# Rows of 4 KB for the first pieces, and neighbourhood attention by two pairs of heads at a time

## The chip, the core and the metric

The program runs on one core of one Trainium2 chip, and the metric is device time in microseconds (us). The core has TensorE (PE, matrix products; its weight loads are PEld), VectorE (DVE), ScalarE (ACT), GpSimd (POOL) and SyncE (SP), which here issues nearly all transfers. The engines take their own instructions in order and wait for one another by semaphores. Products land in PSUM, eight banks of 128 x 512 fp32 here; all else lies in SBUF.

## The reference

A trunk of two layers over 256 tokens of 1024 values, all in fp32. Three mixers work side by side on one input projection:

```python
for l in range(DEPTH):
    x = x + 0.5 * swiglu(rms_norm(x, ffn1_norm[l]), w1, w3, w2)         # hidden width 2816
    z = rms_norm(x, mix_norm[l]) @ w_in[l]                              # 6752 columns
    y_na  = neighborhood_attention(rms_norm(q), rms_norm(k), v, na_rpb[l])   # 8 heads of 64
    y_gla = rms_norm(gla_bidirectional(gq, gk, gv, g_f, g_b)) * silu(gr)     # 4 heads
    y_mla = mla_attention(c_q, c_kv, k_rope, ...)                            # 4 heads
    mixed = gt[0] * (y_na @ w_br_na[l]) + gt[1] * (y_gla @ w_br_gla[l]) + gt[2] * (y_mla @ w_br_mla[l])
    x = x + mixed @ w_out[l]
    x = x + 0.5 * swiglu(rms_norm(x, ffn2_norm[l]), w1, w3, w2)

# neighborhood_attention: tokens on a grid of 4 rows x 64 columns; a block of 16 columns of
# queries sees a band of 32 columns in all 4 rows, and a window of 16 columns inside it
s = einsum('brjqhd,brjkhd->bhrjqk', qg, kg) * d ** -0.5
s = where(mask, s + bias, -1e30)
o = einsum('bhrjqk,brjkhd->brjqhd', softmax(s), vg)
```

## The kernel before, in words

All weights come as "units", 128 partitions by 2048 values (1 MB, rows of 8 KB), in the order of their use, into three buffers called raw. Every unit is split into a high and a low half (hl, four buffers): ScalarE rounds the high half (L143), VectorE takes the rest (L149). Every fp32 product is then three products of halves, and nearly all go through one helper (`mm`, L373). SP has eight transfers under way at most: each waits for the eighth before it.

The main program is a row of projections. After each burst of products on TensorE it calls `tick`, which issues the next splits and lets each small task, a Python generator, go one step. So the order on every engine is fixed when the program is built, and the small products of attention stand between bursts of projections; a visit of TensorE to such a task is what it does there between two bursts. A task that ends a step with `yield n` is called again after n ticks.

Working tiles of 128 x 512 (`s2`) come from a pool of 31 buffers (`S2_BUFS`, L28). A new tile takes the buffer that was freed first, and the instruction that writes it waits for the last reader of the tile that had it. PSUM has four banks for projections (`acc`) and four for the small tasks (`ta`).

The start is written out by hand (`start_first`, L303 to L367). The transposed input xT (eight chunks, called k, of 128 x 256) and the first three units come in 20 transfers of one or two chunks, into 16 tiles of the pool. They are worked off in the groups `(0, 1), (1, 2), (2, 4), (4, 6), (6, 8)` of k: L344 and L347 make the halves of xT with the norm's gain, L352 and L353 those of the units, and per k each unit has six small products (144 in all, 128 x 256), into a bank of its own.

The mixer is at L1116 to L1209. In its order: the MLA and gate inputs, then NA's v, q, k projections; a task normalises q and k (`ev_nqk`: L638 and L640), another transposes them (`na_tr`: L691). `mla_chain` (L851 to L935) has scores for a pair of heads, their softmax (L905, L906, L913), transposes of the probabilities (`p_trans`, L676, split by L247 and L248) and products with v. Then come the projections of GLA's gq and gk (L1133 to L1147), where GLA's gate exponentials (L993 to L995) fall, and four projections of gates, each four bursts of 12 products of 408 columns, among which `na_chain` (L711 to L784) runs, spawned at L1148.

`na_chain` takes the four pairs of heads one at a time, in six steps. Step i loads the bias of pair i + 1 (256 KB), computes scores of pair i (L736, eight small products, 16 records in the trace, into half of two banks), adds the bias and takes the maximum (L743), takes the exponential (L750), divides on GpSimd (L772), transposes pair i - 1 (L778) and multiplies pair i - 2 with v (L761).

Of the kernel before, what the change touches and what calls it, by code (L numbers as in the profile page):

```python
# [46 lines left out]
def body(tc, T):  # L47
# [3 lines left out]
    with ctx:  # L51
# [9 lines left out]
        def s2(shape=(128, 512), dt=F32):  # L61
            return sp.tile(list(shape), dt, name="s2", tag="s2", bufs=S2_BUFS)
# [240 lines left out]
        def start_first():  # L303
# [8 lines left out]
            xr = [s2() for _ in range(4)]  # L312
            rw = [[s2() for _ in range(4)] for _ in range(FIRST_R)]
            groups = ((0, 1), (1, 2), (2, 4), (4, 6), (6, 8))
            at = lambda tiles, a, b: tiles[a // 2][:, a % 2 * 256:a % 2 * 256 + (b - a) * 256]
            for a, b in groups:
                nc.sync.dma_start(out=at(xr, a, b), in_=T["xT"][:, a:b, :])  # L317
                for j in range(FIRST_R):
                    nc.sync.dma_start(out=at(rw[j], a, b), in_=units[j][0][:, a * 256:b * 256])  # L319
# [21 lines left out]
            for a, b in groups:  # L341
                sl = slice(a * 256, b * 256)
                for k in range(a, b):
                    ACT.activation(out=xT[:, :, 0, k, :], in_=at(xr, k, k + 1).rearrange("p (t n) -> p t n", t=2),  # L344
                                   func=AF.Copy, scale=gcol[:, k:k + 1])
                for k in range(a, b):
                    DVE.scalar_tensor_tensor(out=xT[:, :, 1, k, :],  # L347
                                             in0=at(xr, k, k + 1).rearrange("p (t n) -> p t n", t=2),
                                             scalar=gcol[:, k:k + 1], in1=xT[:, :, 0, k, :].bitcast(F32),
                                             op0=ALU.mult, op1=ALU.subtract)  # L350
                for j in range(FIRST_R):
                    ACT.activation(out=hls[j][:, 0, sl], in_=at(rw[j], a, b), func=AF.Copy)  # L352
                    DVE.tensor_tensor(out=hls[j][:, 1, sl], in0=at(rw[j], a, b), in1=hls[j][:, 0, sl].bitcast(F32),  # L353
                                      op=ALU.subtract)
                    for k in range(a, b):
                        part(accs[j], hls[j], k)
# [199 lines left out]
        def mixer(l, norms, after, prefetch):  # L556
# [153 lines left out]

            def na_chain(deps):  # L711
                for d in deps:
                    finish(d)
                bias = {}

                def bias_load(p):
                    if p < 4:
                        bias[p] = s2((128, 2, 2, 128))
                        nc.sync.dma_start(out=bias[p], in_=W["bias"][p])
                bias_load(0)  # L720
                yield 1
                Ps, PTs, sums = {}, {}, {}
                for i in range(4 + 2):
                    if i < 4:
                        bias_load(i + 1)
                        q, k = naT["q", i // 2], naT["k", i // 2]
                        ps = [at_t()[:, :256].rearrange("p (g n) -> p g n", g=2) for _ in range(2)]
                        for g in range(2):
                            for s in range(2):
                                r = slice(s * 64, s * 64 + 64)  # L730
                                for jj in range(2):
                                    j = 2 * g + jj
                                    k0 = min(max(16 * j - 8, 0), 32)
                                    kj = k[r, i % 2, :].rearrange("p (r c) -> p r c", r=4)[:, :, k0:k0 + 32]
                                    o = ps[s][jj * 64:jj * 64 + 64, g, :].rearrange("p (r c) -> p r c", r=4)
                                    mm(o, q[r, i % 2, j * 64:j * 64 + 64], kj, True, True)  # L736
                        m, sm_ = small(4), small(4)
                        P = s2((128, 2, 2, 128))
                        Ps[i], sums[i] = P, sm_
                        b = bias.pop(i)  # L740
                        for s in range(2):
                            for g in range(2):
                                DVE.tensor_tensor_reduce(out=P[:, s, g, :], in0=ps[s][:, g, :], in1=b[:, s, g, :],  # L743
                                                         scale=1.0, scalar=-3.0e38, op0=ALU.add, op1=ALU.max,
                                                         accum_out=m[:, 2 * s + g:2 * s + g + 1])
                        DVE.tensor_scalar(m, m, -1.0, None, op0=ALU.mult)
                        for s in range(2):
                            for g in range(2):
                                e = slice(2 * s + g, 2 * s + g + 1)
                                ACT.activation(out=P[:, s, g, :], in_=P[:, s, g, :], func=AF.Exp,  # L750
                                               bias=m[:, e], accum_out=sm_[:, e])
                    yield 1
                    if i >= 2:
                        p = i - 2
                        ps = at_t()
                        PT = PTs.pop(p)
                        for j in range(4):
                            for s in range(2):
                                h = 2 * p + s
                                o = ps[s * 64:s * 64 + 64, :256].rearrange("p (r c) -> p c r", r=4)  # L760
                                mm(o[:, 16 * j:16 * j + 16, :], nav[j][:, h * 64:h * 64 + 64],  # L761
                                   PT[:, s, j // 2, (j % 2) * 64:(j % 2) * 64 + 64], True, True)
                        if p % 2 == 0:
                            yT["na", p // 2] = (s2(dt=F32R), s2(dt=F32R))
                        hi, lo = yT["na", p // 2]
                        sl = slice((p % 2) * 256, (p % 2) * 256 + 256)
                        split_bank(ps[:, :256], hi[:, sl], lo[:, sl])
                    if i < 4:
                        rs = small(4)
                        DVE.reciprocal(rs, sums[i])  # L770
                        P4 = Ps[i].rearrange("p s g n -> p (s g) n")
                        POOL.tensor_tensor(out=P4, in0=P4, in1=rs[:, :, None].to_broadcast([128, 4, 128]), op=ALU.mult)  # L772
                    if 1 <= i < 5:
                        P = Ps.pop(i - 1)
                        ps = tr_t().rearrange("p (s g n) -> p s g n", s=2, g=2)
                        for s in range(2):
                            for g in range(2):
                                PE.transpose(ps[:, s, g, :], P[:, s, g, :], idt)  # L778
                        PT = PTs[i - 1] = s2((128, 2, 2, 128))
                        if i % 2:  # L780
                            ACT.activation(out=PT, in_=ps, func=AF.Copy)
                        else:
                            DVE.tensor_copy(PT, ps)
                    yield 1  # L784
# [347 lines left out]
            for j, nm in enumerate(("q", "k")):  # L1132
# [236 lines left out]
```

## Time and profile before

| | us |
|---|---|
| median of 3 timed runs (lowest, highest) | 1243.21 (1243.17, 1244.23) |
| profiled execution, its own time | 1244.47 |
| its span | 1242.7 |
| TensorE busy | 1235.9 |
| VectorE busy | 891.0 |
| ScalarE busy | 709.8 |
| GpSimd busy | 219.7 |
| bytes moved | 228.58 MB, mean 184 GB/s |

The span is what the profiler saw of the program; the execution's own time has a little more around it. Busy shares are averages over stages, so a wait is judged where it stands. A timeline row is a run of equal instructions: its start, the time from its first start to its last end, and in brackets how long the engine stood before it and for whom. "Clock" is what the throttle granted TensorE, 1.00 for 2.4 GHz and 0.50 for 1.2 GHz.

### The profile page before, as it was taken

How to read it: one execution, taken by the hardware profiler on the slowest of the kernel's cores; microseconds unless marked ns; L12 is line 12 of the kernel's file. 1: busy time of each engine (PE TensorE's matmuls, PEld its weight loads, DVE VectorE, ACT ScalarE, POOL GpSimd, SP SyncE). 2: the span in 40 equal slices, each digit the busy share in tenths (PEclk: the TensorE clock that was granted, in tenths of full speed). 3: DMA queues.
4: the chain of work that ended last, by engine and by line, in shares of the span. 5: the costliest groups of instructions: out<-in, count | busy, mean ns of one | idle time of the engine just before them, and what ended most of it. 6: DMA issues, size and time to landing. Idle time of an engine off the chain costs nothing.

```text
span 1242.7 us, 18139 instructions
## 1 busy us (share of the span) xinstructions
PE 1235.9 (99%) x7020; PEld 1060.4 (85%) x7020; DVE 891.0 (72%) x1390; ACT 709.8 (57%) x1308; POOL 219.7 (18%) x165
## 2 busy tenths in 40 slices
PE   9999999999999999999999999999999999999998
PEld 8888888889988888888888888888899888888887
DVE  5888736779767778887378886475896677788862
ACT  6655535657665366555365655355686654656541
POOL 0222101132112112220012220021322030122200
PEclk9999999999999999999999999999999999999999
DMA  8655644562543545556355556347526435555560
GB/s 307 232 177 196 239 168 161 181 219 94 198 170 138 201 172 202 177 196 238 136 189 208 203 174 250 120 163 250 175 88 211 170 138 188 191 195 192 181 237 34
DMA packets 39350, 228.58 MB, mean 184 GB/s; under 512 B 5920, under 2 KB 8224, under 8 KB 14816
## 3 DMA queue, kind: packets, MB, share of 16 engines
q1 hardware_dynamic: 39120, 227.42, 52.0%
q8 instruction: 55, 0.90, 0.3%
q14 instruction: 31, 0.25, 0.1%
q10 hardware_dynamic: 144, 0.00, 0.0%
HBM read 224.26 MB, written 1.05 MB: 181 GB/s over the span
## 4 chain that ended last, share of the span: by engine, by line
PE 99%; DMA 0%; SPq 0%; ACT 0%; DVE 0%; issue 0%; DVEq 0%
PE acc L373 80%; PE ta L373 15%; PE ta L691 1%; PE ta L264 1%; DMA s<-in_xT 0%; PE ta L778 0%; PE ta L1199 0%; PE ta L676 0%; SPq L319 0%; PE ta L1014 0%; PE ta L608 0%; PE ta L299 0%; PE ta L469 0%; ACT xT L344 0%; SPq L317 0%; DVE hl L353 0%
## 5 line engine op out<-in xcount | busy, mean ns | idle before, releaser
L149 DVE TENSOR_TENSOR hl<-raw,hl 128x1024 fp32r<-128x1024 f32 (+1 forms) x418 | 560.2, 1381 | 94.1 <-ACT hl L143 83.8
L143 ACT ACTIVATE hl<-raw 128x1024 fp32r<-128x1024 f32 (+1 forms) x418 | 412.9, 1041 | 106.1 <-PE ta L373 87.3
L373 PE MATMUL acc<-xT,hl 128*128 128x256 f32 (+1 forms) x2720 | 466.6, 334 | 0.0
L373 PEld LDWEIGHTS acc<-xT,hl 128*128 128x128 f32 x2720 | 407.9, 188 | 56.3
L373 PE MATMUL acc<-hl,xT 128*128 128x512 f32 (+1 forms) x1584 | 362.9, 384 | 0.0
L373 PEld LDWEIGHTS acc<-hl,xT 128*128 128x128 f32 x1584 | 291.8, 188 | 47.4 <-issue 2.1
L373 PE MATMUL acc<-hl,s 128*128 128x512 f32 x816 | 193.7, 391 | 0.0
L373 PEld LDWEIGHTS acc<-hl,s 128*128 128x128 f32 x816 | 152.6, 188 | 31.7 <-issue 0.3
L483 POOL TENSOR_TENSOR s<-s,rsb 128x512 f32<-128x512 f32 x79 | 109.7, 1388 | 352.1 <-DVE s L482 352.1
L373 PE MATMUL ta<-hl,s 128*128 128x512 f32 (+1 forms) x624 | 148.0, 387 | 0.0
L373 PEld LDWEIGHTS ta<-hl,s 128*128 128x128 f32 x624 | 116.3, 188 | 22.4
L492 ACT ACTIVATE s<-s 128x256 fp32r<-128x256 f32 x82 | 34.0, 417 | 168.1 <-DVE s L490 168.1
L482 DVE TENSOR_TENSOR s<-acc,s 128x256 f32<-128x256 f32 x158 | 59.7, 419 | 58.5 <-ACT s L481 58.5
L569 POOL TENSOR_TENSOR sm<-sm,mhalf 128x4 f32<-128x4 f32 (+2 forms) x24 | 36.7, 1531 | 190.8 <-DVE sm L573 190.8
L285 POOL TENSOR_TENSOR sm<-sm,mhalf 128x1 f32<-128x1 f32 x12 | 14.1, 1175 | 299.0 <-DVE sm L284 299.0
L481 ACT ACTIVATE s<-acc 128x256 f32<-128x256 f32 x158 | 50.6, 372 | 0.0
L247 ACT ACTIVATE s<-ta 128x512 fp32r<-128x512 f32 (+1 forms) x46 | 22.9, 532 | 36.5 <-PE ta L691 16.9
L267 ACT ACTIVATE xT<-ta,gain 128x128 fp32r<-128x128 f32 x80 | 22.8, 368 | 36.3 <-PE ta L264 36.3
L248 DVE TENSOR_TENSOR s<-ta,s 128x512 fp32r<-128x512 f32 (+1 forms) x46 | 26.6, 603 | 22.9 <-ACT s L247 22.5
L488 ACT ACTIVATE s<-s 128x256 f32<-128x256 f32 x82 | 34.2, 419 | 11.5 <-POOL s L483 1.2
L373 PEld LDWEIGHTS ta<-s,s 64*64 64x64 f32 (+3 forms) x720 | 30.4, 145 | 6.9 <-issue 5.9
L373 PE MATMUL ta<-s,s 64*64 64x128 f32 (+4 forms) x720 | 35.9, 261 | 0.0
(160 smaller groups left out, 678.6 us busy)
## 6 DMA issues: line engine op xcount, KB each, us to landing
raw<-in_l_f_w SPq DMA_DIRECT2D x123, 1024.0 KB, 4.8
raw<-in_l_in_g SPq DMA_DIRECT2D x16, 816.0 KB, 4.4
raw<-in_l_in_late SPq DMA_DIRECT2D x8, 1024.0 KB, 4.8
raw<-in_l_out SPq DMA_DIRECT2D x8, 1024.0 KB, 4.8
raw<-in_l_f_up SPq DMA_DIRECT2D x6, 1024.0 KB, 4.8
raw<-in_l_in_m SPq DMA_DIRECT2D x4, 1024.0 KB, 4.8
raw<-in_l_in_gr SPq DMA_DIRECT2D x4, 1024.0 KB, 4.8
raw<-in_l_in_r SPq DMA_DIRECT2D x4, 1024.0 KB, 4.7
```

The costliest lines, as they stand in the source:

```text
L143: ACT.activation(out=hls[j][:, 0, sl], in_=raws[j][:, sl], func=AF.Copy)
L149: DVE.tensor_tensor(out=hl[:, 1, sl], in0=r[:, sl], in1=hl[:, 0, sl].bitcast(F32), op=ALU.subtract)
L247: ACT.activation(out=hi, in_=ps, func=AF.Copy)
L248: DVE.tensor_tensor(out=lo, in0=ps, in1=hi.bitcast(F32), op=ALU.subtract)
L267: ACT.activation(out=xT[:, t, 0, kk, :], in_=ps[:, k * 128:(k + 1) * 128], func=AF.Copy, scale=G[:, kk:kk + 1])
L373: PE.matmul(out=out, lhsT=lhsT, rhs=rhs, start=start, stop=stop, skip_group_check=True)
L481: ACT.activation(out=g[:, j, :], in_=a[j][:, 256:], func=AF.Copy)
L482: DVE.tensor_tensor(out=g[:, j, :], in0=a[j][:, :256], in1=g[:, j, :], op=ALU.add)
L483: POOL.tensor_tensor(out=g, in0=g, in1=rb[:, None, :].to_broadcast([128, 2, 256]), op=ALU.mult)
L488: ACT.activation(out=g[:, 0, :], in_=g[:, 0, :], func=AF.Silu)
L492: ACT.activation(out=o[:, 0, :], in_=g[:, 0, :], func=AF.Copy)
L569: POOL.tensor_tensor(out=r[:, :n], in0=ss[:, :n], in1=mhalf[:, :n], op=ALU.pow)
```

## The change

Three parts.

First, the start. The host lays xT and the first three units into one array `first`, [128, 8, 1024]: per partition and k a row of 4 KB, 256 values of xT and 256 of each unit. Nine transfers (the row of k = 0 in two) bring it into `gates`, which is unused then, and two raw buffers. Everything is then done k by k, with pieces of 256 columns. The fourth unit takes the third raw buffer; the fifth and sixth wait for the two used here.

Second, `na_chain` computes scores for two pairs in one visit (16 products into two whole banks), transposes two pairs in one visit, and multiplies two pairs with v into one full bank, which `ysplit` splits at once.

Third, the bias of all pairs is loaded in the loop of the gq and gk projections, two tiles ahead of each, from the same pool, whose size stays 31.

```diff
-            xr = [s2() for _ in range(4)]
-            rw = [[s2() for _ in range(4)] for _ in range(FIRST_R)]
...
+            homes = [gates[:, k // 2, k % 2 * 1024:k % 2 * 1024 + 1024] for k in range(4)]
+            for _ in range(2):
+                r = wp.tile([128, 2048], F32, name="raw", tag="raw", bufs=RAW_BUFS)
+                homes += [r[:, :1024], r[:, 1024:]]
+            for k in range(8):
+                for sl in (slice(0, 512), slice(512, 1024)) if k == 0 else (slice(0, 1024),):
+                    nc.sync.dma_start(out=homes[k][:, sl], in_=T["first"][:, k, sl])
+            xk = lambda k: homes[k][:, :256].rearrange("p (t n) -> p t n", t=2)
...
+            for k in range(8):
+                sl = slice(k * 256, k * 256 + 256)
...
                 for j in range(FIRST_R):
...
+                    raw = homes[k][:, 256 + j * 256:512 + j * 256]
+                    ACT.activation(out=hls[j][:, 0, sl], in_=raw, func=AF.Copy)
+                    DVE.tensor_tensor(out=hls[j][:, 1, sl], in0=raw, in1=hls[j][:, 0, sl].bitcast(F32),
                                       op=ALU.subtract)
...
+                    part(accs[j], hls[j], k)
...
+                scores(0)
+                soft(0)
+                yield 1
+                soft(1)
+                yield 1
+                norm(0)
+                scores(1)
+                soft(2)
+                yield 1
+                norm(1)
+                soft(3)
+                yield 1
+                norm(2)
+                yield 1
+                for i in range(2):
+                    trans(i)
+                norm(3)
+                yield 2
+                pv(0)
+                yield 1
+                for i in range(2, 4):
+                    trans(i)
+                yield 2
+                pv(1)
+                yield 1
...
             for j, nm in enumerate(("q", "k")):
+                for p in (2 * j, 2 * j + 1):
+                    bias_load(p)
                 hl = unit()
```

How it moves instructions is shown at three places. TensorE in the first layer's four gate projections, before: rows are an operation, its target and sources, its size and count; `acc<-hl,xT` is a projection, `64x128` scores, L778 transposes, `64x16x4` products with v.

```order
L373 MATMUL acc<-hl,xT 128x408 x12
L373 MATMUL ta<-s_2885,s_2497 64x128 x8
L373 MATMUL acc<-hl,xT 128x408 x24
L373 MATMUL ta<-s_2885,s_2497 64x128 x8
L373 MATMUL acc<-hl,xT 128x408 x12
L778 MATMUL ta<-idt,s_3116 128x128 x4
L373 MATMUL acc<-hl,xT 128x408 x12
L373 MATMUL ta<-s_2951,s_2522 64x128 x8
L373 MATMUL acc<-hl,xT 128x408 x12
L373 MATMUL ta<-s_3210,s_2280 64x16x4 x2
...
L778 MATMUL ta<-idt,s_3175 128x128 x4
L373 MATMUL acc<-hl,xT 128x408 x12
L373 MATMUL ta<-s_2951,s_2522 64x128 x8
L373 MATMUL acc<-hl,xT 128x408 x12
```

TensorE there, with the change (L763 are the transposes, two pairs of heads in a row):

```order
L370 MATMUL acc<-hl,xT 128x408 x12
L370 MATMUL ta<-s_2886,s_2490 64x128 x16
L370 MATMUL acc<-hl,xT 128x408 x24
L370 MATMUL ta<-s_2952,s_2515 64x128 x16
L370 MATMUL acc<-hl,xT 128x408 x36
L763 MATMUL ta<-idt,s_3121 128x128 x4
L763 MATMUL ta<-idt,s_3149 128x128 x4
L370 MATMUL acc<-hl,xT 128x408 x24
L370 MATMUL ta<-s_3281,s_2273 64x16x4 x2
...
L370 MATMUL acc<-hl,xT 128x408 x12
L763 MATMUL ta<-idt,s_3198 128x128 x4
L763 MATMUL ta<-idt,s_3230 128x128 x4
L370 MATMUL acc<-hl,xT 128x408 x24
```

The visits for scores go from four to two of double size, and transposes and products with v come in pairs; the runs of projection products between them grow to 36 and 24.

VectorE at the second normalisation of k, before; the numbers behind names tell tiles apart, and the bracket names the engines and transfer queues whose semaphores the instruction waits for:

```order
L638 TENSOR_SCALAR sm_2690<-sm_2690,sm_1868 128x8 [waits Pool_49]
L640 TENSOR_TENSOR s2_2764<-acc_2525,sm_2690 128x512 [waits DVE_49]
L1145 TENSOR_TENSOR s2_2790<-acc_2692,rsb_2018 128x512 [waits PE_49]
...
L670 TENSOR_SCALAR s2_2756<-s2_2756,sm_2800 128x256 [waits DVE_49]
L905 TENSOR_REDUCE sm_2860<-ta_2834 128x2 [waits PE_49]
```

VectorE there, with the change (L637 is what L640 was, L928 what L905 was):

```order
L635 TENSOR_SCALAR sm_2683<-sm_2683,sm_1861 128x8 [waits Pool_49]
L637 TENSOR_TENSOR s2_2761<-acc_2518,sm_2683 128x512 [waits DMAHW2_49,DMAHW1_49,DMAHW6_49,DMAHW0_49,DMAHW7_49,DVE_49,PE_49]
L1170 TENSOR_TENSOR s2_2787<-acc_2689,rsb_2011 128x512
...
L667 TENSOR_SCALAR s2_2753<-s2_2753,sm_2797 128x256 [waits DVE_49]
L928 TENSOR_REDUCE sm_2861<-ta_2835 128x2 [waits PE_49]
```

The order is the same, but the normalisation now also waits for TensorE (PE_49) and for five transfer queues: its output has another buffer of the pool.

ScalarE around the transposed probabilities of MLA (L247) and GLA's exponentials, before:

```order
L247 ACTIVATE s2_2930<-ta_2925 128x512 [waits PE_49]
L247 ACTIVATE s2_2939<-ta_2934 128x512 [waits PE_49]
L143 ACTIVATE hl_2967<-raw_2659 128x816 [waits DMAHW3_49]
L143 ACTIVATE hl_2967<-raw_2659 128x816
L993 ACTIVATE s2_2970<-s2_2679 128x512 [waits DVE_49,PE_49,Activation_49]
...
L247 ACTIVATE s2_3012<-ta_3007 128x512 [waits DVE_49,PE_49]
L247 ACTIVATE s2_3021<-ta_3016 128x512 [waits DVE_49,PE_49,Pool_49]
L993 ACTIVATE s2_3025<-s2_2760 128x512 [waits DVE_49,Pool_49]
```

ScalarE there, with the change (L1016 is what L993 was):

```order
L247 ACTIVATE s2_2931<-ta_2926 128x512 [waits PE_49,Pool_49]
L247 ACTIVATE s2_2940<-ta_2935 128x512 [waits PE_49]
L143 ACTIVATE hl_2968<-raw_2652 128x816 [waits DMAHW0_49]
L143 ACTIVATE hl_2968<-raw_2652 128x816
L1016 ACTIVATE s2_2971<-s2_2672 128x512 [waits DVE_49,PE_49]
...
L247 ACTIVATE s2_3013<-ta_3008 128x512 [waits DVE_49,PE_49,Pool_49]
L247 ACTIVATE s2_3022<-ta_3017 128x512 [waits DVE_49,PE_49]
L1016 ACTIVATE s2_3026<-s2_2757 128x512 [waits PE_49]
```

Again nothing changes places. Both exponentials and the last high half now wait for TensorE or VectorE where they waited for other work or for fewer.

## Rows read from the trace of the kernel before

**Rows 1.** The page's busy times: us (share of span) x instructions.
```profile
PE 1235.9 (99%) x7020; PEld 1060.4 (85%) x7020; DVE 891.0 (72%) x1390; ACT 709.8 (57%) x1308; POOL 219.7 (18%) x165
```

**Rows 2.** Timeline of TensorE, 3:31: start, length, instruction, [idle before].
```profile
4.20 5.28 PE L373 MATMUL ta<-xT,hl 128*128 128x256 f32 x36
11.04 0.50 PE L373 MATMUL ta<-xT,hl 128*128 128x256 f32 x2 [1.55 <-ACT hl L352]
...
26.07 5.12 PE L373 MATMUL acc<-xT,hl 128*128 128x512 f32 x28
```

**Rows 3.** Windows, all engines: busy, (instructions), clock, DMA share, GB/s.
```profile
6.00:12.00 6.00, 4.23 (x34) 3.82 (x33) 3.51 (x9) 3.07 (x7) 0.00 (x0) 1.00 0.84 223
...
17.00:28.00 11.00, 11.00 (x88) 10.77 (x88) 6.58 (x13) 8.75 (x17) 1.10 (x2) 1.00 1.02 419
```

**Rows 4.** ScalarE's, VectorE's lines by form, 2:26: busy us, mean ns | idle.
```profile
L344 ACT ACTIVATE xT<-s,gcol 128x256 fp32r<-128x256 f32 x8 | 3.7, 501 | 3.1 <-DMA s<-in_xT 2.5 <-DMA gcol<-in_gcol 0.7
...
L352 ACT ACTIVATE hl<-s 128x256 fp32r<-128x256 f32 x6 | 2.4, 412 | 1.4 <-DMA s<-in_l_f_w 1.4
...
L347 DVE SCALAR_TENSOR_TENSOR xT<-s,gcol,xT 128x256 fp32r<-128x256 f32 x8 | 3.6, 482 | 5.1 <-ACT xT L344 5.1
...
L353 DVE TENSOR_TENSOR hl<-s,hl 128x256 fp32r<-128x256 f32 x6 | 2.5, 423 | 1.2 <-ACT hl L352 1.2
```

**Rows 5.** Windows, TensorE alone: busy (instructions) clock, DMA share, GB/s.
```profile
12.40:15.70 3.30, 3.30 (x18) 0.50 1.04 400
16.00:25.00 9.00, 9.00 (x78) 1.00 1.02 419
```

**Rows 6.** Timeline of TensorE in the mixer of the first layer.
```profile
320.53 0.67 PE L373 MATMUL ta<-s,s 64*64 64x128 f32 x16
321.13 4.74 PE L373 MATMUL acc<-hl,xT 128*128 128x408 f32 x24
...
332.07 2.49 PE L373 MATMUL acc<-hl,xT 128*128 128x408 f32 x12
334.49 0.69 PE L373 MATMUL ta<-s,s 128*64 128x64 f32 x16
...
341.97 4.71 PE L373 MATMUL acc<-hl,xT 128*128 128x408 f32 x24
346.61 0.69 PE L373 MATMUL ta<-s,s 128*64 128x64 f32 x16
...
383.26 1.60 PE L373 MATMUL ta<-s,s 64*64 64x128 f32 x48
```

**Rows 7.** Waits of VectorE, whole span: total us, times, longest us.
```profile
DVE s L743 <- DMA s<-in_l_bias: 12.7, 4, 4.6
```

**Rows 8.** Timeline of VectorE, 294 to 311 us.
```profile
294.97 0.69 DVE L640 TENSOR_TENSOR s<-acc,sm 128x512 f32<-128x512 f32 x1
295.58 0.68 DVE L1145 TENSOR_TENSOR s<-acc,rsb 128x512 f32<-128x512 f32 x1
...
298.67 0.38 DVE L670 TENSOR_SCALAR s<-s,sm 128x256 f32<-128x256 f32 x1
300.77 0.69 DVE L905 TENSOR_REDUCE sm<-ta 128x2 f32<-128x512 f32 x1 [1.72 <-PE ta L373]
...
309.01 1.28 DVE L248 TENSOR_TENSOR s<-ta,s 128x512 fp32r<-128x512 f32 x2
```

**Rows 9.** Timeline of TensorE, 297 to 312 us.
```profile
298.23 2.51 PE L373 MATMUL ta<-s,s 128*128 128x256 f32 x24
...
305.02 0.66 PE L691 MATMUL ta<-idt,s 128*128 128x128 f32 x4
...
309.99 1.60 PE L373 MATMUL ta<-s,s 128*128 128x256 f32 x12
```

**Rows 10.** Timeline of ScalarE, 299 to 309 us.
```profile
301.74 1.28 ACT L913 ACT_TABLE_LOAD   x1 [0.64 <-DVE sm L906]
...
304.75 0.21 ACT L913 ACTIVATION_READ_ACCUMULATOR s<-ta,sm 128x1 f32 x1
```

More of the change, by code (lines that the diff above doesn't have):

```diff
@@ L311, in start_first @@
             nc.scalar.dma_start(out=gcol, in_=T["gcol"])
-            xr = [s2() for _ in range(4)]
-            rw = [[s2() for _ in range(4)] for _ in range(FIRST_R)]
[L314 to L319, printed above, removed]
+            homes = [gates[:, k // 2, k % 2 * 1024:k % 2 * 1024 + 1024] for k in range(4)]
[6 more added lines that the diff above has]
+            xk = lambda k: homes[k][:, :256].rearrange("p (t n) -> p t n", t=2)
             ACT.activation(out=small(1), in_=ones, func=AF.Copy)
@@ L709, in na_tr, with bias_load @@
                     yield 1
+            bias = {}
+            def bias_load(p):
+                bias[p] = s2((128, 2, 2, 128))
+                nc.sync.dma_start(out=bias[p], in_=W["bias"][p])
             def na_chain(deps):
@@ L713, in na_chain, with scores @@
                     finish(d)
[L714 to L720, printed above, removed]
-                yield 1
[L722 to L727, printed above, removed]
+                yield 1
+                Ps, PTs, sums, sc = {}, {}, {}, {}
+                def scores(G):
+                    ps = sc[G] = [at_t().rearrange("p (w g n) -> p w g n", w=2, g=2) for _ in range(2)]
+                    q, k = naT["q", G], naT["k", G]
+                    for w in range(2):
                         for g in range(2):
@@ L740, in na_chain @@
[L740 to L755, printed above, removed]
+                                    kj = k[r, w, :].rearrange("p (r c) -> p r c", r=4)[:, :, k0:k0 + 32]
@@ new lines, in norm, with trans @@
+                def norm(i):
+                    rs = small(4)
+                    DVE.reciprocal(rs, sums[i])
+                    P4 = Ps[i].rearrange("p s g n -> p (s g) n")
+                    POOL.tensor_tensor(out=P4, in0=P4, in1=rs[:, :, None].to_broadcast([128, 4, 128]), op=ALU.mult)
+                def trans(i):
+                    P = Ps.pop(i)
+                    ps = tr_t().rearrange("p (s g n) -> p s g n", s=2, g=2)
+                    for s in range(2):
+                        for g in range(2):
+                            PE.transpose(ps[:, s, g, :], P[:, s, g, :], idt)
+                    PT = PTs[i] = s2((128, 2, 2, 128))
+                    if i % 2:
+                        DVE.tensor_copy(PT, ps)
+                    else:
+                        ACT.activation(out=PT, in_=ps, func=AF.Copy)
@@ L756, in na_chain, with pv @@
+                def pv(G):
+                    ps = at_t()
+                    for w in range(2):
+                        p = 2 * G + w
                         PT = PTs.pop(p)
@@ L765, in na_chain @@
[L765 to L783, printed above, removed]
@@ L1302, in layout @@
             A[p + f"f{f}_w13"] = _tok(a.reshape(NB, 128, 2048))
-            if (l, f) != (0, "1"):
+            if (l, f) == (0, "1"):
+                A["first"] = _tok(np.concatenate([xT] + [a[c].reshape(128, 8, 256) for c in range(FIRST_R)], 2))
+            else:
                 A[p + f"f{f}_up"] = _tok(a[:2].reshape(2, 128, 2, 4, 256).transpose(2, 1, 3, 0, 4).reshape(2, 128, 2048))
```

49 lines of the change are left out of this document (24 added, 25 removed).

## The prediction

> **What bounds the kernel now.** I read the page's first part, then TensorE's timeline where it is not full, then the work around the places that the change touches. TensorE is busy for 1235.9 of 1242.7 us [rows 1]; the reader should see that nothing else is near it. So an edit counts by what it adds to or takes from TensorE's own row of work: time in which TensorE stands, and time that its instructions need beyond their columns. Nearly all that it stands lies at the start: the products begin at 4.20 us, and 1.55 us goes at 11.04, where the first units' pieces are late [rows 2]. Anywhere else a delay of VectorE or ScalarE is free while TensorE has work queued, and costs its full length beyond that, because TensorE takes its instructions in a fixed order and no later idle time gives anything back.
>
> The sum is made against the profiled execution: 1244.47 us, span 1242.7. The median of the timed runs, 1243.21, lies 1.26 below it, which I take off at the end.
>
> **The start.** Until now the first 144 products end at 26.07 us [rows 2]. From 6 to 12 us, with pieces of 1 to 2 KB per row, the transfers bring 223 GB/s; from 17 to 28 us, when whole units of 1 MB with rows of 8 KB follow, it is 419 [rows 3]. The 4.19 MB of the start now come as rows of 4 KB. At 400 to 419 GB/s [rows 3, 5] a k of 524 KB takes 1.3 us. ScalarE needs at most 0.50 + 3 x 0.41 = 1.74 us per k, VectorE 0.48 + 3 x 0.42 = 1.75 [rows 4]; TensorE's 18 products per k need 2.1 (78 in 9.00 us at full clock [rows 5], 0.115 each; I take 0.12, as records can be missing). So TensorE becomes the bound as soon as it begins, the late pieces at 11.04 go, and the 18 more small instructions on ScalarE and VectorE lie beside it. It begins at about 4.4 (the first piece is somewhat larger), needs 144 x 0.12 = 17.3 us and 0.6 for slower first products (36 took 5.28 us [rows 2], at 0.12 they would have taken 4.3, some of the rest was waiting): end at 22.3, gain 3.8; I take 3.6. In it is the price of the gap: the 3.30 us behind it ran at a granted clock of 0.50, which is 1.2 GHz, and did 1.65 us of work [rows 5]. Bounds: at 223 GB/s a k takes 2.35 us, the eighth lands near 20.6 and its splits and products end near 24.5: still 1.6 gained; at the best 3.9. A loss would need a rate below any in these rows.
>
> The Trainium skill, "DMA: Bandwidth & Descriptors", section "Measured (HBM→SBUF, 128 partitions, SWDGE, issued from GpSimd)", wants 1 MiB or more per transfer, and its fit is 2.0 us plus the bytes at 436 GB/s for each. One behind another, eight pieces of 512 KB would by that estimate take 25.6 us, the first 144 products would end some 1.5 us later than now, and the sum would be 1255.5. By the 223 GB/s, reached with pieces of 128 and 256 KB, several are under way at once here, so I don't follow it; rival B is the like of it without that figure.
>
> **Neighbourhood attention.** Per layer the visits of TensorE to this chain go from nine to six. What a visit costs is read from the runs of 12 and 24 matmuls between visits: 12 take 2.42 us (332.07 to 334.49), 24 take 4.64 (341.97 to 346.61), so 12 more are 2.22 and coming back costs 0.20 [rows 6]. A block of small products has its own fixed price: 16 records take 0.60 to the next start (320.53 to 321.13), 48 take 1.60 with their tail; 32 more are 0.93, 0.029 each, which leaves 0.13 per block [rows 6]. Three returns are 0.60; blocks go from twelve to six, but some stood directly behind another kind, so I count four at 0.13. That is 1.1 per layer, 2.2 in all; bounds 0.6 and 1.4 per layer, 1.2 to 2.8 in all. The exponentials, norms and copies are the same work in other order, beside TensorE; the transposes of pairs 0 and 1 now follow the second pair's norm so closely (I place the norm's end 0.15 us before them) that I add 0.2 per layer; between 0 and 2.
>
> **The bias.** VectorE waited 12.7 us for it, four times in the profile [rows 7]; no wait of TensorE stood behind these, so their end gives nothing. But loading it two projections earlier makes four of the 31 work buffers busy earlier. The pool hands a buffer on when its last reader is done, so everything allocated between the gq projection and the chain gets a buffer that was freed later than before. Following the tiles through the pool, this is where it bites, in both layers alike:
>
> 1. The second k normalisation (L640, now L637) ran at 294.97 and waited only for VectorE itself [rows 8]. Its tile now takes the buffer of the low half of an MLA key, whose last reader is the thirteenth of the 24 score products that start at 298.23: 298.23 + 12 x 0.10 = 299.43, and with its end and the way to VectorE 299.8 [rows 9]. VectorE stands 4.84 us. Behind it are queued one eviction, two splits and the norms, which took from 295.58 to 299.0 = 3.4 us [rows 8]. The reduction of the MLA scores (L905), which ran at 300.77 after waiting 1.72 us for TensorE [rows 8], then runs at 303.8, 3.04 later. The exponentials with their table load start 3.04 later too (304.78 for 301.74), and the last ends at 308.0 instead of 304.96 [rows 10]. It frees the bank into which the transposes of 305.02 go [rows 9], which were only 0.06 behind it. TensorE loses 3.0 us.
> 2. The low half of MLA's head 1 takes the buffer of head 0's low half, read last by the fifth of six products of head 0. The split itself takes 0.60 (two in 1.20 from 309.01 [rows 8]) and stands before head 1's products: with the ways there and back 0.75, of the 1.60 us in which twelve products ran without a break [rows 9]. The same for head 3, high half and low half: 0.75 and 0.63.
> 3. The exponential of the GLA gates (L993, now L1016) waits for the eleventh of the twelve products that began at 309.99 [rows 9]: 309.99 + 10 x 0.12, with 3.8 from above 315. ScalarE stands until then, and the splits queued behind it come late: 0.15.
>
> Together 3.04 + 0.75 + 0.75 + 0.63 + 0.15 = 5.3 us per layer, 10.6 in all. What is queued behind is counted in this; SP's weight transfers wait for older tiles and land ahead of use. Bounds: if the spare time before the transposes is larger than I read by an operation or two, 3 per layer; if the late splits push one another further, 7. Below nothing is excluded, since no instruction leaves that path.
>
> 4. At the start a gap of 1.55 us brought half clock for 3.30 us, a loss of 1.65 [rows 5]. A gap of 3 us stands in the middle of each layer; between 0 and 1.65 each, I take 1.0.
>
> The Trainium skill, "Perfetto Trace Analysis", section "Optimization Strategy", says that a bubble which repeats on the engine that should be full can mean too little memory for the next tile. The trace of before shows none outside the start; by that rule one would look for it here, at the same place in both layers.
>
> **Sum.** -3.6 - 2.2 + 10.6 + 2 x 0.2 + 2 x 1.0 = +7.2: 1251.7 by the profile, 1250.4 as a timed run.
>
> **The rivals.**
> A, faster. The waits for buffers are there but TensorE doesn't feel them: ScalarE or VectorE have more spare time ahead of the transposes than 0.06 us, because the 4.84 us are made up while VectorE would have idled. For it: VectorE is busy 891.0 of 1242.7 us [rows 1]. Against: its idle time ahead of the reduction is 1.72, which I have taken off. Then -3.6 - 2.2 + 0.4 = -5.4: 1237.8. It decides as soon as the wait costs TensorE less than 2.7 us per layer. Chance 0.07; another 0.07 for parts of it, 1241.5 to 1245.5.
> B. The rows of 4 KB come no faster and the gap at 11 us stays: +3.6 less 0 to 2 of the start, 1252 to 1254. For it: no row shows 4 KB. Chance 0.1.
> C. The packed chain waits for its own softmax: transposes and products of pairs 0 and 1 now need two exponentials each, and TensorE stands 1 to 2 us per layer: 1252 to 1254. Chance 0.08.
> The forecast, with its clocks at one or the other level (1248.4 or 1251.7): 0.68.
>
> **The numbers.** The time is the forecast's. A measurement of this kernel tells 0.2% from no change, 2.5 us: 1240.7 and 1245.7 are the limits. Slower: forecast, B, C: 0.86. Within: the part cases, 0.07. Faster: A, 0.07. The range of 8 in 10, 1245.5 to 1254.5, holds the bounds of the buffer waits from 3.5 to 6.5 per layer and both levels of the clock, and leaves rival A out.
>
> **What would show it.** The first 144 products end near 22.3 us, with no gap and no half clock behind 11 us. Six visits per layer, each run of 36 or 24 without a break. A wait of VectorE of nearly 5 us at the second k normalisation, put down to TensorE, and behind it a gap of 3 us on TensorE before transposes, three of 0.6 to 0.75 between the products of MLA heads, all twice. It is wrong if the normalisation starts as early as before, or if TensorE is as full there as it was; then the time is below 1240.

## The result and the profile after

The changed kernel takes 1252.86 us (median of 6 runs, 1251.85 to 1256.16) against 1243.19 before (6 runs, 1242.28 to 1244.61): ratio 1.0079, 95% interval 1.0069 to 1.0089. The forecast was 1250.4, in a range from 1245.5 to 1254.5. The profiled execution took 1252.69 with a span of 1250.9, 8.2 us more than the profiled execution before. One timed run of the last version below took 7044.77 us, far from every other run, and enters no comparison. The page's first part, of the kernel after:

```profile
PE 1236.6 (99%) x7020; PEld 1061.4 (85%) x7020; DVE 890.4 (71%) x1395; ACT 710.4 (57%) x1313; POOL 218.8 (17%) x165
```

TensorE is busy for as long as before, within 0.7 us [rows 1]; the other 7.5 of the 8.2 us are standing. Before, TensorE stood 3.0 us for others. The waits of TensorE after (total us, times, longest):

```profile
PE ta L673 <- ACT s L936: 4.9, 2, 2.4
PE ta L370 <- DVE s L248: 2.2, 4, 1.0
PE ta L308 <- DVE junk L305: 1.2, 1, 1.2
PE ta L370 <- ACT s L247: 1.1, 2, 0.6
PE ta L370 <- ACT hl L350: 0.8, 1, 0.8
PE ta L688 <- ACT s L936: 0.5, 2, 0.3
```

All but two lines come in twos or fours, one or two for each layer, and all of these stand where MLA runs: transposes behind its exponentials L936 (L673 are MLA's own, L688 those of `na_tr`), products behind the splits of the probabilities (L247, L248).

The first link is on VectorE. Its timeline, kernel after (start, length, instruction, idle before):

```profile
297.88 0.69 DVE L637 TENSOR_TENSOR s<-acc,sm 128x512 f32<-128x512 f32 x1 [4.80 <-PE ta L370]
...
301.87 0.68 DVE L928 TENSOR_REDUCE sm<-ta 128x2 f32<-128x512 f32 x1
```

The second k normalisation (L637) stands 4.80 us for TensorE where L640 didn't stand at all [rows 8]. The reduction of the MLA scores (L928) then has no idle time left in front; it had 1.72.

TensorE's timeline before and behind it, kernel after:

```profile
296.36 2.51 PE L370 MATMUL ta<-s,s 128*128 128x256 f32 x24
...
302.17 0.60 PE L673 MATMUL ta<-idt,s 128*128 128x128 f32 x4
305.20 0.66 PE L673 MATMUL ta<-idt,s 128*128 128x128 f32 x4 [2.43 <-ACT s L936]
306.11 0.66 PE L688 MATMUL ta<-idt,s 128*128 128x128 f32 x4 [0.25 <-ACT s L936]
306.52 6.26 PE L370 MATMUL acc<-hl,xT 128*128 128x408 f32 x24
312.62 1.00 PE L370 MATMUL ta<-s,s 128*128 128x256 f32 x7
314.57 0.86 PE L370 MATMUL ta<-s,s 128*128 128x256 f32 x5 [0.95 <-DVE s L248]
...
320.62 1.03 PE L370 MATMUL ta<-s,s 128*128 128x256 f32 x6
322.22 0.38 PE L370 MATMUL ta<-s,s 128*128 128x256 f32 x1 [0.57 <-ACT s L247]
322.95 0.86 PE L370 MATMUL ta<-s,s 128*128 128x256 f32 x5 [0.34 <-DVE s L248]
...
325.96 1.10 PE L370 MATMUL ta<-s,s 64*64 64x128 f32 x32
```

The wait of L637 ends where the order of the tiles had put it: the thirteenth of the 24 products that start at 296.36 begins near 296.36 + 12 x 0.10 = 297.6, and L637 runs at 297.88.

The rest is to be compared with [rows 9]: 2.43 us in front of the second four transposes of L673, 0.25 in front of L688, then 0.95, 0.57 and 0.34 between the products of the MLA heads, which ran twelve without a break before. From 298.80 to 325.96 TensorE needs 27.16 us, where the same work took 19.86 (300.67 to 320.53). Of the 7.3 us lost there, 1.5 are no wait: the 24 products of 408 columns behind the long gap take 6.10 us (306.52 to 312.62), where 24 without a break took 4.56 in the kernel before (305.43 to 309.99). The gaps in brackets add up to 4.54, and stopping and starting again makes up the other 1.2: twelve products with one gap of 0.95 span 2.81 (312.62 to 315.43), where they took 1.60 without. The windows of TensorE, kernel after, for this run and for the same run in the second layer (us, busy, count, granted clock, DMA share, GB/s):

```profile
306.50:312.60 6.10, 6.10 (x27) 0.72 0.37 115
927.40:931.90 4.50, 4.50 (x26) 1.00 0.20 29
```

The clock fell behind the gap in the first layer (0.72 on average, part of the run at 1.2 GHz), and not behind a gap of the same length in the second.

The start, TensorE, kernel after:

```profile
4.69 3.23 PE L370 MATMUL ta<-xT,hl 128*128 128x256 f32 x18
8.68 15.69 PE L370 MATMUL ta<-xT,hl 128*128 128x256 f32 x126 [0.76 <-ACT hl L350]
24.20 5.81 PE L370 MATMUL acc<-xT,hl 128*128 128x512 f32 x32
```

The first 144 products end at 24.20 instead of 26.07 [rows 2]. There is still a gap, of 0.76 us. ScalarE's timeline there, kernel after:

```profile
7.81 0.51 ACT L345 ACTIVATE xT<-gates,gcol 128x256 fp32r<-128x256 f32 x1 [2.56 <-DMA gates<-in_first]
```

The second piece of 512 KB lands at 7.8 us, after 2.56 us in which ScalarE has nothing; from there on the pieces come fast enough that ScalarE never stands for one again. What had been moved by then (us, TensorE's busy time and count, granted clock, DMA share, GB/s), kernel after:

```profile
0.50:5.70 5.20, 4.53 (x12) 1.00 0.71 221
0.50:7.80 7.30, 6.63 (x26) 1.00 0.78 248
6.00:12.00 6.00, 5.24 (x40) 1.00 1.00 366
```

By 5.7 us 1.15 MB have come, a little more than the first two pieces (1.05 MB), and by 7.8 us 1.81 MB, over three pieces; the second is whole only then. In the trace the sixteen reports of its landing come one by one from 5.2 to 7.8 us. So bytes of later pieces arrive ahead of its last ones, and it is late for another reason than a low rate.

The chain of neighbourhood attention, TensorE, kernel after:

```profile
332.71 6.98 PE L370 MATMUL acc<-hl,xT 128*128 128x408 f32 x36
...
365.42 1.03 PE L1037 MATMUL ta<-idt,s 128*128 128x128 f32 x8
```

Between the first scores and the GLA transposes behind the chain TensorE needs 39.46 us (325.96 to 365.42), where it needed 40.66 (320.53 to 361.19): 1.2 us less per layer, with no wait in it.

### The profile page after: what moved, and what is told of

The parts are those of the page before. It is cut to its first block, busy times and chain, and to the rows that moved or that the text cites. A ratio compares the mean times of both kernels' runs of the same rounds, so it can differ in the third digit from the quotient of the medians.

```text
span 1250.9 us, 18129 instructions
## 1 busy us (share of the span) xinstructions
PE 1236.6 (99%) x7020; PEld 1061.4 (85%) x7020; DVE 890.4 (71%) x1395; ACT 710.4 (57%) x1313; POOL 218.8 (17%) x165
## 3 DMA queue, kind: packets, MB, share of 16 engines
HBM read 224.26 MB, written 1.05 MB: 180 GB/s over the span
## 4 chain that ended last, share of the span: by engine, by line
PE 97%; DVE 1%; ACT 1%; DMA 0%; issue 0%; SPq 0%; DVEq 0%; ACTq 0%
PE acc L370 79%; PE ta L370 15%; PE ta L688 1%; PE ta L264 1%; DMA gates<-in_first 0%; DVE hl L149 0%; PE ta L1224 0%; PE ta L763 0%; ACT s L936 0%; DVE s L248 0%; ACT L936 0%; PE ta L673 0%; PE ta L1037 0%; PE ta L605 0%; DVE s L667 0%
## 5 line engine op out<-in xcount | busy, mean ns | idle before, releaser
L248 DVE TENSOR_TENSOR s<-ta,s 128x512 fp32r<-128x512 f32 (+1 forms) x42 | 26.4, 647 | 36.4 <-ACT s L247 32.2
L247 ACT ACTIVATE s<-ta 128x512 fp32r<-128x512 f32 (+1 forms) x42 | 22.6, 564 | 33.1 <-PE ta L688 17.4
```

The source lines that it names most:

```text
L247: ACT.activation(out=hi, in_=ps, func=AF.Copy)
L248: DVE.tensor_tensor(out=lo, in0=ps, in1=hi.bitcast(F32), op=ALU.subtract)
```

## The experiments

All are compared with runs of the kernel before on the same chip: 1243.28 in the first group of four, 1243.12 in the second, 1243.02 in the third. Each group had another chip; these medians lie within 0.3 us, so versions of different groups can be compared to about that.

**Bias in an idle tile.** The bias is loaded as early as in the change, but holds no tile of the pool.

```diff
-                bias[p] = s2((128, 2, 2, 128))
-                nc.sync.dma_start(out=bias[p], in_=W["bias"][p])
+                c = (824, 1232, 1488, 1744)[p]
+                o = gates[:, :, c:c + 256]
+                nc.sync.dma_start(out=o, in_=W["bias"][p].rearrange("p s g n -> p s (g n)"))
+                bias[p] = o.rearrange("p s (g n) -> p s g n", g=2)
```

> The changed kernel, its bias loaded at the same two places ahead of the chain, but into columns 824 to 1999 of the gates tile, which nobody uses until the second gate projection is done; so no tile of the pool is held for it. Theory P (the four pool tiles held early cause the waits): the second k normalisation starts without its 4.8 us wait, the gaps of TensorE ahead of the MLA transposes and between the heads' products go (5.8 and 5.4 us in the two layers), and with them the half clock of 1.5 us: 1252.9 - 11.2 - 1.5 = about 1240, within 1.5. Rival Q (the early transfers or the new order of the chain cause the gaps, not the buffers): all stays, 1251 to 1254.

1239.76 (1239.22 to 1240.64), ratio to the kernel before 0.997, interval 0.9958 to 0.9981. TensorE's waits, all of them:

```profile
PE ta L370 <- ACT hl L350: 1.2, 1, 1.2
PE ta L308 <- DVE junk L305: 1.2, 1, 1.2
```

VectorE at the second k normalisation and the reduction behind it:

```profile
292.96 0.69 DVE L637 TENSOR_TENSOR s<-acc,sm 128x512 f32<-128x512 f32 x1
...
298.74 0.69 DVE L930 TENSOR_REDUCE sm<-ta 128x2 f32<-128x512 f32 x1 [1.71 <-PE ta L370]
```

TensorE at the second transposes of `na_tr` and behind:

```profile
303.00 0.66 PE L688 MATMUL ta<-idt,s 128*128 128x128 f32 x4
303.41 4.72 PE L370 MATMUL acc<-hl,xT 128*128 128x408 f32 x24
307.96 1.60 PE L370 MATMUL ta<-s,s 128*128 128x256 f32 x12
```

The normalisation starts at once, the reduction again waits 1.71 us for TensorE as in [rows 8], there is no gap in front of the transposes, the 24 products take 4.55 us and the twelve products of two heads 1.60, as in [rows 9]. 13.1 us go with four held tiles, though the transfers are as early and the chain is in the new order. Theory P held to half a microsecond.

**Bias late again, from the pool.**

```diff
-                for p in (2 * j, 2 * j + 1):
-                    bias_load(p)
...
+                bias_load(0)
                 yield 1
+                bias_load(1)
...
                 soft(0)
+                bias_load(2)
                 yield 1
                 soft(1)
+                bias_load(3)
```

> The changed kernel with the bias loaded inside the chain again, from the pool: pairs 0 and 1 at its start, 2 and 3 behind the first scores. Theory P: no wait for a buffer is left ahead of the chain, 1240 within 1.5, as with the bias in the gates tile. Rival Q of the order: if the new order of the chain makes the gaps, 1251 to 1254. A third way: VectorE now waits for the late bias as it did before the change (12.7 us in four waits), and since scores of two pairs hold two whole banks, TensorE might stand for it: up to 2 us per layer more, 1242 to 1244.

1240.54 (1238.41 to 1242.82), ratio 0.9977, interval 0.9968 to 0.9985. The only wait of TensorE in the chain (L765 are the transposes):

```profile
PE ta L765 <- POOL s L758: 0.3, 1, 0.3
```

VectorE's wait for the bias:

```profile
DVE s L744 <- DMA s<-in_l_bias: 9.3, 2, 4.9
```

So VectorE does stand up to 4.9 us for the late bias, twice in this profile, and TensorE stands 0.3 us for the chain, once. In the timed runs the early loading is worth 0.8 us at most (1240.54 against 1239.76), and the two intervals overlap. The rival of the order and the third way both fall. The profiled execution did take 1242.77, but through its start: its gap there is 2.03 us, the granted clock is 0.63 from 12.0 to 15.4 us, and the first 144 products end at 26.46, against 24.04 in the version with the bias in the gates tile.

**Early bias alone, in the kernel before.**

```diff
-                        bias_load(i + 1)
...
             for j, nm in enumerate(("q", "k")):
+                for p in (2 * j, 2 * j + 1):
+                    bias_load(p)
```

> The kernel before with one part of the change alone: the bias of all pairs loaded in the loop of the gq and gk projections, from the same 31 tiles. Theory P: the same waits as in the changed kernel, 5.4 us per layer in gaps of TensorE and up to 1.5 for the clock: 1243.2 + 11.2 + 0 to 3 = 1254.4 to 1257. Rival Q of the order: without the new order the gaps stay away, 1243 within 1.

1255.52 (1254.64 to 1256.49), ratio 1.0096, interval 1.0083 to 1.011, in the middle of the forecast. TensorE's waits in MLA (L676 are the transposes, L911 the exponentials here):

```profile
PE ta L676 <- ACT s L911: 4.9, 2, 2.4
PE ta L373 <- DVE s L248: 1.9, 4, 0.6
...
PE ta L373 <- ACT s L247: 1.1, 2, 0.6
```

But for the small wait of L688 and 0.3 us these are the waits of the changed kernel, with neither the new start nor the new chain. The early bias alone costs 12.2 us.

**One tile more in the pool.**

```diff
-S2_BUFS = 31
+S2_BUFS = 32
```

> The changed kernel with 32 tiles in the pool for 31, which is all that memory holds. Theory P by the order of the tiles: the wait moves one instruction back, from the second k normalisation to the eviction of gq behind it (+4.2 us there for 4.8), the gap ahead of the transposes shrinks by about 0.6 to 2.4, head 1's low half no longer waits, head 3's still does: some 3.5 us per layer for 5.6, so 1248 to 1250. If one tile more does away with all of it (a pool that was short by one), 1240. If the pool has no part in it, 1252.9.

1248.52 (1246.04 to 1249.45), ratio 1.0037, interval 1.0023 to 1.005. VectorE at the normalisation and the eviction of gq behind it:

```profile
293.80 0.69 DVE L637 TENSOR_TENSOR s<-acc,sm 128x512 f32<-128x512 f32 x1
298.55 0.69 DVE L1170 TENSOR_TENSOR s<-acc,rsb 128x512 f32<-128x512 f32 x1 [4.06 <-PE ta L370]
```

TensorE's timeline:

```profile
305.27 0.65 PE L673 MATMUL ta<-idt,s 128*128 128x128 f32 x4 [1.84 <-ACT s L936]
306.18 0.66 PE L688 MATMUL ta<-idt,s 128*128 128x128 f32 x4 [0.26 <-ACT s L936]
...
311.15 1.60 PE L370 MATMUL ta<-s,s 128*128 128x256 f32 x12
...
319.54 0.86 PE L370 MATMUL ta<-s,s 128*128 128x256 f32 x5 [0.61 <-DVE s L248]
```

With one tile more the wait has moved one instruction back, as the order of the tiles said: L637 starts at once, L1170 stands 4.06 us. The gap at the transposes is 1.84 + 0.26, the products of the first two heads run through (1.60), those of the next two still stand 0.61. No half clock follows here in the first layer (311.15 less 306.60 is 4.55 for the 24 products between); in the second these take 5.60. The time is in the forecast range of theory P. So the pool is short by more than one tile, and the loss follows which tile takes whose buffer.

**The new start alone, in the kernel before.** The start of the change, with chain and bias of the kernel before.

```diff
+            homes = [gates[:, k // 2, k % 2 * 1024:k % 2 * 1024 + 1024] for k in range(4)]
...
+                    nc.sync.dma_start(out=homes[k][:, sl], in_=T["first"][:, k, sl])
```

> The kernel before with the new start alone (rows of 4 KB, k by k); chain and bias as before. By the prediction's term the first 144 products end near 22.3 us and the time is 1239.7. By the profiles so far they end at 24.0 to 26.5, because the second piece lands only at 7.6 to 8.5 us while the first engines are done with it at 5.1; against the 24.4 and 26.1 of the two profiles with the old start this gives 0 to 2: 1241 to 1243.5. The chain's part is then the rest of the 3.5 us that the version with the bias in the gates tile has gained.

1242.66 (1241.07 to 1244.69), ratio 0.9992, interval 0.9983 to 1.0001: not told apart from no change. Its start on TensorE:

```profile
9.38 15.69 PE L370 MATMUL ta<-xT,hl 128*128 128x256 f32 x126 [1.74 <-ACT hl L350]
24.91 5.81 PE L370 MATMUL acc<-xT,hl 128*128 128x512 f32 x32
```

The gap was 1.74 us here and the end 24.91. Together with the profiles above, where the new start ends at 24.04 to 26.46 and the old one at 26.07 and 24.37, this shows that both starts vary by about 2 us from one profiled execution to another, and that the 1.87 us between the two profiles are partly chance. The prediction's 3.6 us for the start are not there: the interval allows 2.1 at most.

**The start's array laid out piece by piece.**

```diff
-                    nc.sync.dma_start(out=homes[k][:, sl], in_=T["first"][:, k, sl])
+                    nc.sync.dma_start(out=homes[k][:, sl], in_=T["first"][k, :, sl])
```

> The version with the bias in the gates tile, the array of the start laid out piece by piece, so that each piece of 512 KB is contiguous in memory and its rows no longer lie 32 KB apart. Theory L (the layout in memory slows some of the transfer engines): the second piece lands near 5.3 us instead of 7.6 to 8.5, TensorE has no gap, the first 144 products end at 22.3 and the time is 1238. Theory E (some engine is slow in the first 8 us whatever it reads): nothing changes, 1239.8 within 0.7.

1238.46 (1238.31 to 1240.0), ratio 0.9963, interval 0.9951 to 0.9976. TensorE at the start:

```profile
8.08 15.69 PE L370 MATMUL ta<-xT,hl 128*128 128x256 f32 x126 [0.84 <-ACT hl L350]
23.61 5.81 PE L370 MATMUL acc<-xT,hl 128*128 128x512 f32 x32
```

A gap of 0.84 us is left, the end is 23.61. The second piece landed at 7.2. By itself the layout is no more than a small part: theory L, which had it at 5.3, falls, though the time is the one that it named. The profiled execution, 1239.36, is the second slowest of five, so the others may have a smaller gap. The intervals of this kernel and of the one it was made from overlap.

**Rows of 1 KB for the first two pieces.**

```diff
             for k in range(8):
-                for sl in (slice(0, 512), slice(512, 1024)) if k == 0 else (slice(0, 1024),):
-                    nc.sync.dma_start(out=homes[k][:, sl], in_=T["first"][:, k, sl])
+                n = 256 if k < 2 else 1024
+                for c in range(0, 1024, n):
+                    nc.sync.dma_start(out=homes[k][:, c:c + n], in_=T["first"][:, k, c:c + n])
```

> The version with the bias in the gates tile, the first two pieces of the start in four transfers each (rows of 1 KB), the others as rows of 4 KB. In the old start with such rows the second k had landed by 5.8 us. Theory R (long rows hold the late engine up): the second k lands near 5.8, the third near 9, the gap moves to the third piece and shrinks to 1 us or none: end of the first products 22.5 to 24, time 1238 to 1239. Theory E (a slow engine whatever the rows): the second k lands at 7 to 8.5 and nothing changes, 1239.8 within 0.7.

1239.8 (1239.21 to 1242.28), ratio 0.9976, interval 0.9967 to 0.9985. ScalarE, at the end of the second piece and the start of the third:

```profile
5.66 1.32 ACT L351 ACTIVATE hl<-gates 128x256 fp32r<-128x256 f32 x3
9.61 0.51 ACT L346 ACTIVATE xT<-gates,gcol 128x256 fp32r<-128x256 f32 x1 [2.63 <-DMA gates<-in_first]
```

The second piece is there by 6.6 us, not at 7.6 to 8.5, so it isn't that nothing can land earlier, and theory E falls, though its time came out. But the third, the first with long rows, then makes ScalarE stand for 2.63 us, and the whole gains nothing. Theory R was right that the second piece would come earlier and the third late, and wrong about the time. Its 5.8 us was misread, too: in the old start only the first parts of the second k were there by then, and ScalarE stood for the others until 7.03.

**Rows of 2 KB for all pieces.** The same edit with `n = 512` for every k.

> The version with the bias in the gates tile, every piece of the start in two transfers with rows of 2 KB. Theory R (row length): between the two, the second k lands near 6.7 and the later ones, with only 2 MB under way, no earlier than before: 1239 within 1. Theory E: 1239.8 within 0.7. If half the bytes under way starve the engines as in the old start (223 GB/s from 6 to 12 us), TensorE waits for the third to fifth k and it is slower, 1241 to 1242.

1238.48 (1238.08 to 1238.55), ratio 0.9959, interval 0.9946 to 0.9971. TensorE at the start:

```profile
4.56 17.85 PE L371 MATMUL ta<-xT,hl 128*128 128x256 f32 x144
22.24 5.81 PE L371 MATMUL acc<-xT,hl 128*128 128x512 f32 x32
```

ScalarE there:

```profile
5.71 0.51 ACT L346 ACTIVATE xT<-gates,gcol 128x256 fp32r<-128x256 f32 x1 [0.59 <-DMA gates<-in_first]
6.12 1.23 ACT L351 ACTIVATE hl<-gates 128x256 fp32r<-128x256 f32 x3
```

The first half of the second piece is there at 5.7, the other half by about 6.6 (the three splits take 1.23 us, 1.01 without a wait), near the 6.7 of theory R. ScalarE stands 0.59 us and little more, and TensorE has no gap: the 144 products end at 22.24. This is the start as it was forecast, to 0.1 us, with half the row. All five runs lie below all runs of the version that it was made from (1239.22 and more). That 2 MB under way would starve the engines was wrong. The rate until 5.7 us (a window as above) is the changed kernel's:

```profile
0.50:5.70 5.20, 4.53 (x15) 1.00 0.76 221
```

So with as many bytes in, half of the second piece is whole here that is not whole there.

**The first piece in four, the others in two.** `n = 256 if k == 0 else 512`.

> The version with halves (bias in the gates tile, pieces in two transfers with rows of 2 KB), the first piece alone in four with rows of 1 KB. With such rows the first k landed 0.5 us earlier and TensorE began at 4.21 instead of 4.56. If TensorE stays fed behind it, the first products end 0.3 earlier, at 21.9, and the time is 1238.1. If the second piece, now issued two transfers later (each about 0.45 us), comes late, a gap of up to 1 us opens, with half clock behind it: 1239 to 1240.5.

1238.47 (1237.72 to 1238.96), ratio 0.9959, interval 0.9948 to 0.9971. TensorE begins at 4.21, as expected, but the 144 products end at 22.72 and not at 21.9: the third piece is late here (ScalarE stands 1.36 us until 8.49), though its rows are of 2 KB. Neither of the two forecasts came; the time is the same as with halves.

**The same, laid out piece by piece.** Both edits are shown above.

> The same with the array laid out piece by piece. The layout took 0.4 to 1.3 us off the landing of the second piece when it was one transfer. With halves TensorE has no gap left for that to fill, so no change: within 0.6 of the version beside it; 1238.1 if that one has no gap, and if it has one, this closes part of it.

1238.6 (five of six runs from 1238.35 to 1238.74), ratio 0.996, interval 0.9948 to 0.9973. No difference in the time, as expected. But the layout did not bring the second piece earlier here: its first half came at 6.38 instead of 5.69, and TensorE has a gap of 0.40 us. The four versions at 1238.5 to 1238.6 are 4.4 to 4.7 us faster than the kernel before and about 14.3 faster than the changed one.

## Why the prediction was right, and where it was off

The sum, term by term; the two profiles, and for each part the median of runs that isolates it:

| term | forecast | two profiles | runs of parts |
|---|---|---|---|
| start | -3.6 | -1.9 | -0.5 (start alone) |
| chain (visits, and the packed softmax) | -1.8 | -2.4 | -2.9 (bias in the gates tile against start alone) |
| waits for buffers | +10.6 | +11.2 | +13.1 with the next line (change against bias in the gates tile) |
| half clock behind them | +2.0 | +1.5 | |
| sum | +7.2 | +8.4 | +9.7 |

In the last column each part is the difference of two neighbouring versions, so they add up to the measured time whatever they are. The column of the profiles, whose spans differ by 8.2, is lower because the profiled execution before was 1.26 us slower than its median and the one after 0.17 faster.

**The waits for buffers.** Right as a mechanism and nearly in size. The first step, L637, was to stand until 299.8, 4.84 us: it stood 4.80. It was to cost TensorE 3.04: in both layers it cost 2.96 (in the first, L688 runs at 306.11 for 305.02, though the work before it runs 1.87 us earlier). The steps behind it were to cost 2.3 per layer; they cost 2.8 in the first layer and 2.5 in the second (0.60 for the first of them there instead of 0.95). The third step was the weak one: 0.15 was put down for ScalarE's late exponential, and it seems to be part of the larger gaps; the runs don't take it apart. That the early bias causes all of it is shown three ways: without the held tiles it goes, in the kernel before it comes, and with another size of pool it moves. Rival A needed a cost to TensorE under 2.7 us per layer, and it is 2.96: the 1.72 us were all that VectorE had, and they are gone.

The Trainium skill, "Perfetto Trace Analysis", section "Optimization Strategy", says that a bubble which repeats on the engine that should be full can mean too little memory for the next tile. The trace agrees: the same 2.43 or 2.44 us in front of the same transposes in both layers, and nothing there once four tiles fewer are held.

**The start.** This term failed: 3.6 us were forecast, and the new start alone gains 0.5. The step is "At 400 to 419 GB/s [rows 3, 5] a k of 524 KB takes 1.3 us. [...] So TensorE becomes the bound as soon as it begins". It lets the pieces land one behind another at a mean rate, and takes that rate from 12 us and later for the first 8. What ScalarE and TensorE need per k was right: with rows of 2 KB the end is 22.24, forecast 22.3. But the second transfer of 512 KB was whole at 7.2 to 8.6 us in six profiles, where 1.3 us behind the first, whole at 4.2, would be 5.5. By 7.8 us 1.81 MB had come in the changed kernel, enough for three pieces.

The bound of 223 GB/s [rows 3] would have given 24.5, and 24.20 was measured; that is luck. At 223 every piece would have come late, but 366 GB/s were moved from 6 to 12 us, and only the second piece was late. Rival B had the start's gain at 0 to 2, which is right, and its time, 1252 to 1254, came out. Its picture is only half right: a gap stays, of 0.76 to 2.03 us and before 9.5 us in the five profiles with this layout, but the rows of 4 KB do come faster than the old ones. The time stayed inside the range because terms were off in opposite ways: the start +3.1, the buffers with their clock +0.5, the chain -1.1, together the 2.5 us between 1250.4 and 1252.86.

**The chain.** Three visits fewer and blocks of double size were to save 1.1 us per layer, less 0.2 for the softmax. TensorE saved 1.2 between the same two places, and had no wait for the packed softmax, except 0.3 us once when the bias was late. So the 0.2 were not needed, and rival C falls.

**The clock.** Half clock behind the gap was taken at 1.0 per layer. It was 1.5 in the first layer and 0 in the second of the same execution; with the early bias alone the mean was 0.86 in the run behind the gap in both layers, and with 32 tiles it was 0 in the first layer and 1.0 in the second. So the price per gap was within its bounds, and whether it is paid differs from gap to gap.

## What to carry to other kernels

Loading something earlier from a shared pool of tiles is not free when memory, not transfer time, is scarce: the price stands where the next instruction takes a buffer of another reader, far from the load, and the order of the tiles tells beforehand where. Here the thing wanted early fitted into a tile that was idle at that time, and the loss of 9.7 us turned into a gain of 3.5. A mean rate of the transfers doesn't tell when one piece is whole: at the start, with several under way, the second piece was whole only when more than three had come in. When a piece is whole has to be read from what waits for it.

## What the hardware showed that was not expected

- At the start of the program two transfers of 256 KB with rows of 2 KB landed at 5.7 and about 6.6 us, where one transfer of 512 KB with rows of 4 KB, issued at about the same time, landed at 7.2 to 8.6, with the same 221 GB/s until 5.7 us in two of these kernels; later, both come at 400 GB/s or more. The Trainium skill, "DMA: Bandwidth & Descriptors", section "Measured (HBM→SBUF, 128 partitions, SWDGE, issued from GpSimd)", asks for 1 MiB or more per transfer to reach three quarters of the peak rate. In this place, with SP issuing and several transfers under way, the trace differs: transfers of 256 KB moved 400 GB/s from 8 to 12 us, and the first products ended at 22.24 us with them, at 24.20 with the larger ones. Why the long rows are late there is not settled, and row length and size of transfer were not varied apart: laying the array out piece by piece moved the landing to 7.2 us only, and with the first piece in four transfers a third piece with rows of 2 KB came as late as 8.49.
- A gap of 2.4 us on TensorE brought 1.2 GHz behind it in the first layer and not in the second of one execution, with the same instructions on either side; with 32 tiles, and a gap of 1.84, it was the other way round.
